# First 16 tokens' values with stacked high and low parts, and a later sub-norm, in a two-block f32 stack

## The chip, the cores and the metric

The kernel runs on one core of a Trainium2 chip. The metric is the device time of one launch in microseconds (us), as a median over runs. All matrix products are float32 products that are made on TensorE from pairs of float32r tiles: a high part and a low part of each operand, and three of the four products of the parts (high by high, high by low, low by high).

## The reference, cut to what matters

Two blocks run one after the other. Block 1 is two layers of ffn, token mixing and ffn on 512 tokens; block 2 puts 16 meta tokens in front and is two layers of a mixer and an ffn on 528 tokens. The model width is 1024. The change touches the values and forget logits of block 2's mixer, and the sub-norm of block 1's differential attention.

```
# block 2, mixer_sublayer (twice)
u = rms_norm(h, pre_g)                              # 528 x 1024
z = einsum("bld,de->ble", u, w_in)
q, k, v, f_logit, a_val, a_gate, sc_b, sc_c, sc_x = split(z)
log_f = log_sigmoid(f_logit + b_forget)             # 8 heads
y_attn = forgetting_attention(q, k, v, log_f)       # v: 528 x 512
a = causal_depthwise_conv(a_val * sigmoid(a_gate), a_dw_w) + a_dw_b   # 31 taps
...
# block 1, token_mixing (twice)
o_b = rmsnorm(diff_attention(...), subln_g) * (1.0 - lambda_init)
```

## The kernel before, in words

The residual lives transposed, 128 features by tokens, as eight chunks of the width (`KC` = 8). Block 2's 528 tokens are two halves: `H[0]` holds tokens 0 to 271 (the 16 meta tokens first), `H[1]` tokens 272 to 527. The normalized input of a sublayer is `xh` and `xl`, its high and low part, one pair of tiles for each chunk and half.

**Weights** are loaded by SyncE in 128x512 pieces (`wr`); ScalarE makes the high part (`wh`, L200) and VectorE the low part (`wl`, L201). A product is three matmuls for each chunk (`mm3`, L222 to L224; for values L778 to L780, where the tokens are the stationary operand and the weights stream).

**Values in mixer 2.** `gen_v(g)` (L1176) makes the values of four heads at a time. For g=0 the weight slice is 264 columns wide, 256 of values and 8 of forget logits; for g=1 it is 256. It hands a list of token blocks to `v_gen`: first the 16 meta tokens, then four blocks of 128. For each block and chunk there are three matmuls into one PSUM bank; then ScalarE writes the high part of the values (L787), VectorE the low part (L788), and for g=0 `forget` adds the bias to the logits (`lft`, L1166). So the 16 meta tokens cost 8 times 3 matmuls for each g, and there are two g and two layers. From the forget logits come `lf` (L1174), five small transposes (L1198), a scan (L1200), and the decay rows that go through DRAM (`fdram`, `dec`, L1202 and L1208) to the first scores (L1242).

**Order.** The program is a set of Python generators. They yield after each group of matmuls the TensorE time that they estimate (109 per matmul of values), and a planner takes the next piece from another generator when it is owed: the 31 taps of the depthwise convolution (L1333, L1337, one VectorE instruction each) are paced this way beside the values, and so are the filler matmuls of the next sublayer and the weight loads. Where a generator yields less, all that is paced by it comes earlier or later in the order of every engine.

**Sub-norm of block 1.** The differential attention's output is normed at the end of its units. Reciprocals are spread to 64 columns each (`bR`); after a yield, for each of four tiles two transposes on TensorE (L1063) bring them beside the output, VectorE scales (L1066), ScalarE and VectorE make the high and low parts (L1068, L1069). `SUBLN` says how many units of the other attention heads go by before each of the two parts is taken.

**GpSimd** (POOL) does next to nothing: a few memsets, and at the very end of the program eight residual additions (L370).

Of the kernel before, what the change touches and what calls it, by code (L numbers as in the profile page):

```python
# [9 lines left out]
F32 = mybir.dt.float32  # L10
F32R = mybir.dt.float32r
BF16 = mybir.dt.bfloat16
ACTF = mybir.ActivationFunctionType
ALU = mybir.AluOpType
# [3 lines left out]
KC = 8  # L18
# [4 lines left out]
HB = 272  # L23
# [17 lines left out]
END = (1050, 570)  # L41
CUT1, CUT2 = (7,), (5, 7)
OUT1, OUT2 = (5, 6, 7, 4, 3, 0, 1, 2), (0, 1, 4, 5, 2, 7, 6, 3)
SUBLN = (1, 2)
LATE = (3, 6, 7)
LAST = ("ffn3", DEPTH - 1)

# [32 lines left out]
def block_stack_kernel(ctx: ExitStack, tc: tile.TileContext, x_in, meta_in, vec_in, lam_in, wup1, wdn1, wqk1,  # L80
                       wv1, wo1, strip_a, wqk2, wv2, wcv2, wpw2, wo2, wup2, wdn2, c_ident, c_stripb,
                       c_cmask, c_fmask, c_sel, c_selc, out, n_sub=99):
    nc = tc.nc
    act, dve, pe, pool = nc.scalar, nc.vector, nc.tensor, nc.gpsimd
# [10 lines left out]
    def half(dt=F32, name="h"):  # L95
        return hp.tile([128, HB], dt, tag="h", name=name)
# [12 lines left out]
    def bank(tag, shape=(128, 512)):  # L109
        return ps.tile(list(shape), F32, tag=tag, bufs=bank_tags[tag], name="ps_" + tag)  # L110
# [4 lines left out]
    def lbank():  # L115

        lin[0] += 1
        return bank(lin[1][lin[0] % len(lin[1])])
# [8 lines left out]
    zeroc = one.tile([128, 1], F32, name="zeroc")  # L127
# [4 lines left out]
    def V(name, l, i=0, n=1):  # L132
        c = VCOL[name, l] + i
        return vec[:, c:c + n]
# [43 lines left out]
    def wunit(*key, back=0):  # L178

        assert plan[head[0]][0] == key, (plan[head[0]][0], key)  # L180
        head[0] += 1
        fetch(head[0] + AHEAD - back)
        return ready.pop(head[0] - 1)
# [19 lines left out]
    def fetch(to):  # L203
        while head[1] < min(to, len(plan)):
            for _ in load():
                pass
# [37 lines left out]
    class Whole:  # L244

        i, n, g, c = None, TALL - T0, slice(T0, TALL), slice(0, TALL - T0)
# [29 lines left out]
    def first_operand(opnd, h, g, wait):  # L276

        yield wait
        for c in range(KC):
            xs, gs = xT[:, c, h.g], g(c)  # L280
            xh, xl = opnd.tiles(c)
            act.activation(out=xh[:, h.g], in_=xs, func=ACTF.Copy, scale=gs)
            dve.scalar_tensor_tensor(out=xl[:, h.g], in0=xs, scalar=gs, in1=xh[:, h.g].bitcast(F32),  # L283
                                     op0=ALU.mult, op1=ALU.subtract)
            opnd.x[h.i, c] = (xh, xl)
            yield T_CH
        acc = None
        for c in range(KC):
            sq = half(name="sq")
            act.activation(out=sq[:, h.c], in_=xT[:, c, h.g], func=ACTF.Square)  # L290
            if acc is None:
                acc = sq
            else:
                dve.tensor_tensor(out=acc[:, h.c], in0=acc[:, h.c], in1=sq[:, h.c], op=ALU.add)
            yield T_SQ
        got = []
        yield from rb_steps(h, acc, got)
        opnd.set_rb(h, *got)
# [469 lines left out]
    def v_gen(opnd, us, tbs, width, get_v, extra=None, done=None):  # L768
        us = us() if callable(us) else us
        for (h, a, b, rcol) in tbs:  # L770
            n = b - a
            p = lbank()
            for c in range(KC):
                xh, xl = opnd.at(c)
                xsl = (slice(None), slice(a, b))
                wsl = (slice(None), slice((c % 4) * width, (c % 4 + 1) * width))
                wh, wl = us[c // 4]
                pe.matmul(out=p[:n, :width], lhsT=xh[xsl], rhs=wh[wsl], start=c == 0, stop=False)  # L778
                pe.matmul(out=p[:n, :width], lhsT=xh[xsl], rhs=wl[wsl], start=False, stop=False)
                pe.matmul(out=p[:n, :width], lhsT=xl[xsl], rhs=wh[wsl], start=False, stop=c == KC - 1)  # L780
                yield 3 * 109
            vt = get_v(a)
            r = opnd.r[h.i][:n, rcol:rcol + 1]
            vv = vt[:n].rearrange("p (q a b) -> p q a b", a=2, b=64)
            hi, lo = vv[:, :, 0, :], vv[:, :, 1, :]
            src = p[:n, 0:256].rearrange("p (q b) -> p q b", b=64)
            act.activation(out=hi, in_=src, func=ACTF.Copy, scale=r)  # L787
            dve.scalar_tensor_tensor(out=lo, in0=src, scalar=r, in1=hi.bitcast(F32), op0=ALU.mult,  # L788
                                     op1=ALU.subtract)
            if extra:  # L790
                extra(a, n, p, r)
            if done:
                done(a)
# [33 lines left out]
    def mixer1(l, opnd, gpost, nxt):  # L827
        H = HALF[1]
        li = 0.8 - 0.6 * math.exp(-0.3 * l)
        with ExitStack() as st:  # L830
# [261 lines left out]
            def with_subln(us):  # L1092

                sg = subln()
                for i, (needs, u) in enumerate(us):
                    def wrapped(u=u, i=i):
                        next(u)
                        yield
                        next(u)
                        if i in SUBLN:  # L1100
                            next(sg, None)
# [28 lines left out]
    def mixer2(l, opnd, gpost, nxt):  # L1130
        H = HALF[2]
        TB = [(0, 16), (16, 144), (144, 272), (272, 400), (400, 528)]
        with ExitStack() as st:
# [35 lines left out]
            def log_sigmoid():  # L1169
# [3 lines left out]
                act.activation(out=e, in_=e, func=ACTF.Ln, bias=1.0)  # L1173
                dve.scalar_tensor_tensor(out=f, in0=t, scalar=0.0, in1=e, op0=ALU.min, op1=ALU.subtract)  # L1174

            def gen_v(g):  # L1176
                w = 264 if g == 0 else 256
                us = lambda: [wunit("mix2", l, "v", g, j) for j in range(2)]

                def get(a):  # L1180
                    tb = 0 if a == 0 else (a - 16) // 128 + 1
                    vt[g, tb] = t = mp.tile([128, 512], F32R, tag="L", bufs=26, name="v")
                    return t
                tbs = [(H[0], 0, 16, 2)] + [(h, a, b, j) for h in H for j, (a, b) in enumerate(h.tb)]
                return v_gen(opnd, us, tbs, w, get, forget if g == 0 else None)

            def vsl(h, tb):
                m = TB[tb][1] - TB[tb][0]
# [307 lines left out]
            def run(gen, every):  # L1496

                ns = 0
                for d in gen:
                    ns += d  # L1500
                    while ns >= every:
                        fill(1)
                        ns -= every

            run(gen_v(0), TAP_V)
            log_sigmoid()
            first = pair(0)
# [6 lines left out]
            fl.add(("qk", 1), pair(1))  # L1514
            fl.add(("qk", 2), pair(2))
            fl.add(("v", 1), gen_v(1))
            fl.add("sc0", sc_branch(0))

# [11 lines left out]
            op = out_proj(2, l, ytile, gpost, nxt, OUT2, CUT2, y_done, scored)  # L1530
            fl.add("out", until_tail(op))
            us = []
# [87 lines left out]
    def blk_of(kind, l):  # L1620
        return 3 if (kind, l) == LAST else 2 if kind in ("mix2", "ffn3") else 1
# [3 lines left out]
    cur, opnd = None, Operand()  # L1625
# [17 lines left out]
    g = lambda c: V(pre[k0], l0, c)  # L1643
    start = iter([("steps", first_operand(opnd, h, g, T_B * h.i)) for h in HALF[blk_of(k0, l0)]])
    for i, (kind, l) in enumerate(subs):
        if i + 1 < len(subs):
            k2, l2 = subs[i + 1]
            nopnd = Operand()
            nxt = (HALF[blk_of(k2, l2)], nopnd, lambda c, k2=k2, l2=l2: V(pre[k2], l2, c))
        else:  # L1650
            nopnd = None
            nxt = (HALF[blk_of(kind, l)], None, None)
        gp = lambda c, kind=kind, l=l: V(post[kind], l, c)
        if kind == "mix1":
            gen = mixer1(l, opnd, gp, nxt)
        elif kind == "mix2":
            gen = mixer2(l, opnd, gp, nxt)
        elif kind == "ffn3":
            gen = ffn(blk_of(kind, l), (kind, l), opnd, gp, nxt, lambda f, l=l: V("ffn_conv_w_2", l, 3 * f, 3),
                      1 if blk_of(kind, l) == 3 else 2)  # L1660
        else:
            gen = ffn(1, (kind, l), opnd, gp, nxt)
        weave([cur or start, gen])
        if cur is None:
            prepare(*load_rest(g0))
        next(gen)
        cur, opnd = gen, nopnd
# [134 lines left out]
```

## Time and profile before

| | |
|---|---|
| median of 3 runs | 3420.25 us (3419.7 to 3424.2) |
| the profiled execution | 3422.85 us |
| its span, first to last instruction | 3421.1 us |
| mean granted TensorE clock | 0.991 of full |
| TensorE busy | 3381.2 us (99%) |
| weight loads on TensorE | 2992.2 us (87%) |
| VectorE busy | 2060.9 us (60%) |
| ScalarE busy | 1524.9 us (45%) |
| GpSimd busy | 8.9 us in 28 instructions |

How to read it: a row of the timeline is start, duration, engine, line, operation, output<-inputs, shape and count, with idle time and its releaser in brackets. Matmuls of a row overlap (each is shown with about 0.28 us while the next starts 0.12 us later), so what one costs is the distance between starts. A row of the windows is one stretch with the busy time and the number of instructions of each engine, the granted clock, and what the DMA moved. Names of tiles are the program's.

### The profile page before, as it was taken

The numbers are of one execution on the slowest core, as the hardware profiler recorded it, in microseconds if no ns is written. First come the engines' busy times: TensorE is split into PE (matmuls) and PEld (weight loads), VectorE is DVE, ScalarE is ACT, GpSimd is POOL, SyncE is SP. The second block draws the span as 40 slices with busy tenths as digits, with TensorE's granted clock in tenths as the row PEclk, the third lists the DMA queues.
The fourth block names the chain that finished last, engine by engine and source line by source line (L and its number), as shares of the span: only waits on it lengthen the run. The fifth ranks groups of instructions, "written<-read, shape, count | busy, mean of one in ns | idle before, by whom it ended". The sixth has DMA issues, their size and how long they took to land.

```text
span 3421.1 us, 55949 instructions
## 1 busy us (share of the span) xinstructions
PE 3381.2 (99%) x21765; PEld 2992.2 (87%) x21765; DVE 2060.9 (60%) x4433; ACT 1524.9 (45%) x3342; POOL 8.9 (0%) x28
## 2 busy tenths in 40 slices
PE   9999999999999999999999999999999999999998
PEld 8888987988888888987988898879999998799998
DVE  6442688744336442788744349768774397677743
ACT  6332566633234332566633235555443345664432
POOL 0000000000000000000000000000000000000000
PEclk9999999999999999999999999999999999999999
DMA  4223222232323223222223322102222221122222
GB/s 144 98 91 97 79 74 75 69 103 95 93 87 99 96 92 96 79 76 63 87 93 98 91 89 88 48 32 96 91 93 86 85 85 57 35 93 93 93 90 78
DMA packets 165817, 291.40 MB, mean 85 GB/s; under 512 B 19456, under 2 KB 36896, under 8 KB 165552
## 3 DMA queue, kind: packets, MB, share of 16 engines
q1 hardware_dynamic: 163648, 287.13, 26.4%
q8 instruction: 171, 2.80, 0.3%
q10 hardware_dynamic: 1904, 0.70, 0.1%
q14 instruction: 94, 0.77, 0.1%
HBM read 285.62 MB, written 2.13 MB: 84 GB/s over the span
## 4 chain that ended last, share of the span: by engine, by line
PE 88%; DVE 7%; ACT 3%; issue 1%; DMA 0%; SPq 0%; POOLq 0%; ACTq 0%; DVEq 0%
PE ps_acc L222 10%; PE ps_acc L223 10%; PE ps_acc L224 10%; PE ps_s L223 8%; PE ps_s L222 8%; PE ps_s L224 8%; PE ps_x L222 4%; PE ps_x L223 4%; PE ps_x L224 4%; PE ps_o L223 4%; PE ps_o L222 4%; PE ps_o L224 4%; PE ps_o L819 2%; PE ps_s L802 2%; DVE y L1337 1%
## 5 line engine op out<-in xcount | busy, mean ns | idle before, releaser
L200 ACT ACTIVATE wh<-wr 128x512 fp32r<-128x512 f32 (+2 forms) x1068 | 616.0, 615 | 1084.6 <-PE ps_acc L223 468.7
L201 DVE TENSOR_TENSOR wl<-wr,wh 128x512 fp32r<-128x512 f32 (+2 forms) x1068 | 693.1, 673 | 476.8 <-ACT wh L200 465.1
L222 PE MATMUL ps_acc<-xh,wh 128*128 128x256 f32 (+3 forms) x1608 | 533.5, 332 | 2.4 <-DVE qt L748 1.5
L223 PE MATMUL ps_acc<-xl,wh 128*128 128x256 f32 (+3 forms) x1608 | 521.4, 324 | 0.0
L224 PE MATMUL ps_acc<-xh,wl 128*128 128x256 f32 (+3 forms) x1608 | 521.1, 324 | 0.0
L223 PE MATMUL ps_s<-xl,wh 128*128 128x512 f32 (+3 forms) x1088 | 360.2, 331 | 2.8 <-DVE xl L283 0.8
L222 PE MATMUL ps_s<-xh,wh 128*128 128x512 f32 (+3 forms) x1088 | 357.5, 329 | 1.8 <-DVE z L531 1.6
L224 PE MATMUL ps_s<-xh,wl 128*128 128x512 f32 (+3 forms) x1088 | 356.5, 328 | 0.1
L222 PEld LDWEIGHTS ps_acc<-xh,wh 128*128 128x128 f32 x1608 | 306.4, 191 | 32.4 <-DVE qt L748 3.3
L224 PEld LDWEIGHTS ps_acc<-xh,wl 128*128 128x128 f32 x1608 | 306.0, 190 | 25.9 <-issue 1.5
L223 PEld LDWEIGHTS ps_acc<-xl,wh 128*128 128x128 f32 x1608 | 306.9, 191 | 22.1
L223 PEld LDWEIGHTS ps_s<-xl,wh 128*128 128x128 f32 x1088 | 204.8, 188 | 27.1 <-DVE xl L378 6.8
L222 PEld LDWEIGHTS ps_s<-xh,wh 128*128 128x128 f32 x1088 | 204.7, 188 | 22.2 <-DVE z L531 2.0
L224 PEld LDWEIGHTS ps_s<-xh,wl 128*128 128x128 f32 x1088 | 204.5, 188 | 18.7 <-DVE wl L201 0.3
L222 PE MATMUL ps_x<-xh,wh 128*128 128x256 f32 (+2 forms) x600 | 202.4, 337 | 0.0
L224 PE MATMUL ps_x<-xh,wl 128*128 128x256 f32 (+2 forms) x600 | 199.5, 333 | 0.0
L223 PE MATMUL ps_x<-xl,wh 128*128 128x256 f32 (+2 forms) x600 | 199.3, 332 | 0.0
L223 PE MATMUL ps_o<-xl,wh 128*128 128x512 f32 (+3 forms) x544 | 179.0, 329 | 1.0
L222 PE MATMUL ps_o<-xh,wh 128*128 128x512 f32 (+3 forms) x544 | 177.5, 326 | 0.1
L224 PE MATMUL ps_o<-xh,wl 128*128 128x512 f32 (+3 forms) x544 | 177.4, 326 | 0.0
L223 PE MATMUL ps_acc<-hl,wh 128*128 128x256 f32 (+1 forms) x528 | 168.5, 319 | 0.0
L222 PE MATMUL ps_acc<-hh,wh 128*128 128x256 f32 (+1 forms) x528 | 168.1, 318 | 0.0
(347 smaller groups left out, 7574.9 us busy)
## 6 DMA issues: line engine op xcount, KB each, us to landing
wr<-in_wup_dram SPq DMA_DIRECT2D x528, 256.0 KB, 2.8
wr<-in_wdn_dram SPq DMA_DIRECT2D x192, 256.0 KB, 2.7
wr<-in_wqk_dram SPq DMA_DIRECT2D x96, 256.0 KB, 2.8
wr<-in_wdn_dram SPq DMA_DIRECT2D x96, 192.0 KB, 2.6
wr<-in_wo_dram SPq DMA_DIRECT2D x64, 256.0 KB, 2.7
wr<-in_wv_dram SPq DMA_DIRECT2D x40, 256.0 KB, 2.9
wr<-in_wcv_dram SPq DMA_DIRECT2D x40, 256.0 KB, 2.8
dec<-fdram SPq DMA_DIRECT2D x16, 264.0 KB, 4.2
```

The costliest lines, as they stand in the source:

```text
L200: act.activation(out=hi[:, a:b], in_=raw[:, :b - a], func=ACTF.Copy)
L201: eng.tensor_tensor(out=lo[:, a:b], in0=raw[:, :b - a], in1=hi[:, a:b].bitcast(F32), op=ALU.subtract)
L222: pe.matmul(out=o, lhsT=wh[wsl], rhs=xh[xsl], start=start, stop=False)
L223: pe.matmul(out=o, lhsT=wh[wsl], rhs=xl[xsl], start=False, stop=False)
L224: pe.matmul(out=o, lhsT=wl[wsl], rhs=xh[xsl], start=False, stop=stop)
L802: pe.matmul(out=o, lhsT=a[R, qs], rhs=b[R, ks], start=j == 0, stop=j == 2 and mask is None)
L819: pe.matmul(out=o[:, q0:], lhsT=v, rhs=p[j], start=kb == 0 and j == 0, stop=kb == n - 1 and j == 1)
L1337: dve.scalar_tensor_tensor(out=y[:, s:], in0=t[0][:, :TALL - s], scalar=w[:, 30 - s:31 - s], in1=y[:, s:], op0=ALU.mult, op1=ALU.add))
```

## The change

The matmuls of the 16 meta tokens leave `v_gen`. A new generator, `first_v`, builds for each chunk a stationary operand of 48 columns, in which the 16 columns of the tokens' high part stand at 0 and the 16 of the low part at 32, with zeros between them and after; a matmul of that operand with the weights' high part gives high by high in rows 0 to 15 of the bank and low by high in rows 32 to 47. A second matmul, of the first 16 columns with the weights' low part, adds high by low to rows 0 to 15. So there are two matmuls for each chunk in place of three. GpSimd builds the operand: two fills with zero (128x272) and 16 copies (128x16) for each call, and `gen_v` is called four times. The two row groups are then added: ScalarE copies rows 32 to 47 to `vm`, VectorE adds rows 0 to 15, and the high and low parts of the values and the forget logits are made from `vm`. The generator yields 2*109 for each chunk. The second edit sets `SUBLN` from (1, 2) to (1, 3): the second part of the sub-norm is taken one unit later, in both layers of block 1.

```diff
--- before.py
+++ after.py
@@ -41,7 +41,7 @@
 END = (1050, 570)
 CUT1, CUT2 = (7,), (5, 7)
 OUT1, OUT2 = (5, 6, 7, 4, 3, 0, 1, 2), (0, 1, 4, 5, 2, 7, 6, 3)
-SUBLN = (1, 2)
+SUBLN = (1, 3)
 LATE = (3, 6, 7)
 LAST = ("ffn3", DEPTH - 1)
 
@@ -1173,16 +1173,51 @@
                 act.activation(out=e, in_=e, func=ACTF.Ln, bias=1.0)
                 dve.scalar_tensor_tensor(out=f, in0=t, scalar=0.0, in1=e, op0=ALU.min, op1=ALU.subtract)
 
+            def first_v(us, w, get, extra):
+
+                us, xm = us(), [half(F32R, "xm") for _ in range(2)]
+                for i in range(2):
+                    pool.tensor_copy(out=xm[i], in_=zeroc.to_broadcast([128, HB]))
+                    for c in range(4):
+                        for k in range(2):
+                            pool.tensor_copy(out=xm[i][:, 48 * c + 32 * k:48 * c + 32 * k + 16],
+                                             in_=opnd.at(4 * i + c)[k][:, 0:16].bitcast(F32))
+                p = lbank()
+                for c in range(KC):
+                    x = xm[c // 4][:, 48 * (c % 4):48 * (c % 4) + 48]
+                    wsl = (slice(None), slice((c % 4) * w, (c % 4 + 1) * w))
+                    wh, wl = us[c // 4]
+                    for rows, y in ((48, wh), (16, wl))[::-1 if c == KC - 1 else 1]:
+                        pe.matmul(out=p[:rows, :w], lhsT=x[:, :rows], rhs=y[wsl], start=c == 0 and rows == 48,
+                                  stop=c == KC - 1 and rows == 48)
+                    yield 2 * 109
+                t = half(name="vm")
+                act.activation(out=t[0:16, :w], in_=p[32:48, :w], func=ACTF.Copy)
+                dve.tensor_tensor(out=t[0:16, :w], in0=t[0:16, :w], in1=p[0:16, :w], op=ALU.add)
+                r = opnd.r[0][:16, 2:3]
+                vv = get(0)[:16].rearrange("p (q a b) -> p q a b", a=2, b=64)
+                src = t[:16, 0:256].rearrange("p (q b) -> p q b", b=64)
+                act.activation(out=vv[:, :, 0, :], in_=src, func=ACTF.Copy, scale=r)
+                dve.scalar_tensor_tensor(out=vv[:, :, 1, :], in0=src, scalar=r, in1=vv[:, :, 0, :].bitcast(F32),
+                                         op0=ALU.mult, op1=ALU.subtract)
+                if extra:
+                    extra(0, 16, t, r)
+
             def gen_v(g):
                 w = 264 if g == 0 else 256
-                us = lambda: [wunit("mix2", l, "v", g, j) for j in range(2)]
+                made = []
+
+                def units_of():
+                    made[:] = made or [wunit("mix2", l, "v", g, j) for j in range(2)]
+                    return made
 
                 def get(a):
                     tb = 0 if a == 0 else (a - 16) // 128 + 1
                     vt[g, tb] = t = mp.tile([128, 512], F32R, tag="L", bufs=26, name="v")
                     return t
-                tbs = [(H[0], 0, 16, 2)] + [(h, a, b, j) for h in H for j, (a, b) in enumerate(h.tb)]
-                return v_gen(opnd, us, tbs, w, get, forget if g == 0 else None)
+                tbs = [(h, a, b, j) for h in H for j, (a, b) in enumerate(h.tb)]
+                ex = forget if g == 0 else None
+                return itertools.chain(first_v(units_of, w, get, ex), v_gen(opnd, units_of, tbs, w, get, ex))
 
             def vsl(h, tb):
                 m = TB[tb][1] - TB[tb][0]
```

On TensorE, at the start of mixer 2's values in layer 0, the order before has the meta tokens' block first (`ps_o`, 24 matmuls of 16 rows, of which the first three stand here, the rest repeats them), behind the last product of the convolution's inputs:

```order
L222 MATMUL ps_x<-xh,wh 128x256
L223 MATMUL ps_x<-xl,wh 128x256
L326 MATMUL ps_t<-onec,sq 128x1 x2
L224 MATMUL ps_x<-xh,wl 128x256
L778 MATMUL ps_o<-wh,xh 16x264
L779 MATMUL ps_o<-wl,xh 16x264
L780 MATMUL ps_o<-wh,xl 16x264
```

Now a block of 128 tokens comes first and the 16 matmuls of `xm` follow it; these are the end of that block, two transposes of a reciprocal (L341), and the first chunk of `xm`:

```order
L778 MATMUL ps_acc<-wh,xh 128x264
L779 MATMUL ps_acc<-wl,xh 128x264
L780 MATMUL ps_acc<-wh,xl 128x264
L341 MATMUL ps_t<-ident,R 128x128 x2
L1191 MATMUL ps_o<-wh,xm 48x264
L1191 MATMUL ps_o<-wl,xm 16x264
```

Twenty-four rows became sixteen, and they moved behind the 24 of the first 128-token block.

On TensorE, in the first mixing layer of block 1, the sub-norm's four pairs of transposes stood between the score matmuls of a unit of 128 columns (L802):

```order
L802 MATMUL ps_s<-kh,qh 128x128 x2
L1063 MATMUL ps_t<-ident,bR 128x128 x2
L802 MATMUL ps_s<-kl,qh 128x128 x2
L1063 MATMUL ps_t<-ident,bR 128x128 x2
L802 MATMUL ps_s<-kh,ql 128x128 x2
L1063 MATMUL ps_t<-ident,bR 128x128 x2
L222 MATMUL ps_acc<-xh,wh 128x512
```

Now they stand behind the scores of the next unit, between products of the weights and the first of the values' products (L819):

```order
L802 MATMUL ps_s<-kh,ql 128x256 x2
L222 MATMUL ps_acc<-xh,wh 128x512
L1063 MATMUL ps_t<-ident,bR 128x128 x2
L223 MATMUL ps_acc<-xl,wh 128x512
L224 MATMUL ps_acc<-xh,wl 128x512
L1063 MATMUL ps_t<-ident,bR 128x128 x2
L222 MATMUL ps_acc<-xh,wh 128x512
L223 MATMUL ps_acc<-xl,wh 128x512
L224 MATMUL ps_acc<-xh,wl 128x512
```

The same rows move in the second layer.

On VectorE, between the convolution's input products and the forget gate (`lf`) of layer 0, the order before begins with both gatings of the convolution's input (L1330, two tiles) and the first tap (L1333):

```order
L1330 TENSOR_TENSOR av<-av,ag 128x528 x2
L1333 TENSOR_SCALAR y<-av,vec 128x528
L788 SCALAR_TENSOR_TENSOR v<-ps_o,rt,v 16x4x64
L1337 SCALAR_TENSOR_TENSOR y<-av,vec,y 128x527
L1166 SCALAR_TENSOR_TENSOR lft<-ps_o,rt,vec 16x8
```

Now only one gating stands there, and the addition of the row groups (L1196) is new; lines of the new kernel behind L1176 are 35 higher:

```order
L1365 TENSOR_TENSOR av<-av,ag 128x528
L1196 TENSOR_TENSOR vm<-vm,ps_o 16x264
L1368 TENSOR_SCALAR y<-av,vec 128x528
L1166 SCALAR_TENSOR_TENSOR lft<-vm,rt,vec 16x8
L1372 SCALAR_TENSOR_TENSOR y<-av,vec,y 128x527
L1201 SCALAR_TENSOR_TENSOR v<-vm,rt,v 16x4x64
```

The second gating now comes behind the first scores of the layer, and one tap fewer stands ahead of those scores.

## Rows read from the trace of the kernel before

**Rows 1.** Page, parts 1 and 4: busy time by engine; chain that ended last
```profile
PE 3381.2 (99%) x21765; PEld 2992.2 (87%) x21765; DVE 2060.9 (60%) x4433; ACT 1524.9 (45%) x3342; POOL 8.9 (0%) x28
...
PE 88%; DVE 7%; ACT 3%; issue 1%; DMA 0%; SPq 0%; POOLq 0%; ACTq 0%; DVEq 0%
```

**Rows 2.** Windows: us, busy by engine (instructions), PEclk, DMA share, GB/s
```profile
570.00:575.00 5.00, 4.10 (x24) 2.62 (x23) 4.81 (x12) 2.74 (x7) 0.00 (x0) 1.00 0.16 57
1585.00:1590.00 5.00, 4.56 (x27) 3.37 (x25) 3.98 (x11) 4.07 (x11) 0.00 (x0) 1.00 0.29 95
2050.00:2060.00 10.00, 9.56 (x68) 8.27 (x68) 9.19 (x28) 5.17 (x14) 0.00 (x0) 1.00 0.05 17
2083.00:2102.00 19.00, 18.67 (x150) 17.43 (x149) 18.78 (x36) 10.02 (x19) 0.34 (x2) 1.00 0.40 139
```

**Rows 3.** Timeline of PE: 16-token values of layer 0, g=0, then g=1
```profile
2067.66 0.28 PE L778 MATMUL ps_o<-wh,xh 128*16 128x264 f32 x1
...
2070.84 0.29 PE L778 MATMUL ps_acc<-wh,xh 128*128 128x264 f32 x1
...
2071.57 0.28 PE L778 MATMUL ps_acc<-wh,xh 128*128 128x264 f32 x1
...
2134.16 0.29 PE L778 MATMUL ps_acc<-wh,xh 128*16 128x256 f32 x1 [0.25 <-DVE qt L748]
...
2136.98 0.28 PE L778 MATMUL ps_acc<-wh,xh 128*128 128x256 f32 x1
```

**Rows 4.** Waits of PE over the whole span: us in total, times, longest
```profile
PE ps_t L1063 <- DVE ptl L906: 1.2, 2, 0.8
...
PE ps_o L1295 <- ACT sc L1251: 2.2, 1, 2.2
...
PE ps_t L1198 <- DVE lf L1174: 0.4, 2, 0.2
```

**Rows 5.** POOL instructions by form: count, busy us, mean ns, idle before
```profile
L370 POOL TENSOR_TENSOR xT<-xT,f 128x256 f32<-128x256 f32 x8 | 6.3, 786 | 621.1 <-DVE f L356 614.9 <-issue 6.2
L1596 POOL TENSOR_SCALAR vec<-vec 128x8 f32<-128x8 f32 x4 | 1.0, 289 | 4.0 <-DMA vec<-in_vec_dram 4.0
...
L1565 POOL MEMSET warm<- 128x272 f32 x1 | 0.3, 324 | 0.0
...
L1558 POOL MEMSET selz<- 128x16 f32 x1 | 0.1, 112 | 0.0
```

**Rows 6.** Groups of DVE instructions by form, 2050 to 2061 us
```profile
L378 DVE SCALAR_TENSOR_TENSOR xl<-xT,vec,xh 128x256 fp32r<-128x256 f32 x8 | 3.8, 473 | 0.7 <-ACT xh L386 0.7
L362 DVE TENSOR_TENSOR xT<-xT,f 128x256 f32<-128x256 f32 x8 | 3.3, 415 | 0.0
```

**Rows 7.** Timeline of DVE in mixer 2, layer 0
```profile
2072.44 1.33 DVE L1330 TENSOR_TENSOR av<-av,ag 128x528 f32<-128x528 f32 x2 [0.21 <-ACT ag L1329]
...
2074.15 0.47 DVE L788 SCALAR_TENSOR_TENSOR v<-ps_o,rt,v 16x256 fp32r<-16x256 f32 x1
2074.54 0.75 DVE L1337 SCALAR_TENSOR_TENSOR y<-av,vec,y 128x527 f32<-128x527 f32 x1
...
2081.96 1.29 DVE L201 TENSOR_TENSOR wl<-wr,wh 128x512 fp32r<-128x512 f32 x2 [1.19 <-ACT wh L200]
```

**Rows 8.** Timeline of SP and DVE: decay loads and their first use
```profile
2095.06 1.77 SPq L1208 DMA_DIRECT2D dec<-fdram  x4
...
2102.46 0.15 DVE L1242 CUSTOM_DVE_ANT_0 sc<-ps_s,dec 16x16 f32<-16x16 f32 x1
```

**Rows 9.** Timeline of POOL and DVE at the end of the program
```profile
3404.53 0.79 POOL L370 TENSOR_TENSOR xT<-xT,f 128x256 f32<-128x256 f32 x1 [614.07 <-DVE f L356]
...
3405.30 0.42 DVE L370 TENSOR_TENSOR xT<-xT,f 128x256 f32<-128x256 f32 x1
```

**Rows 10.** Windows at the end of layer 0's mixer 2
```profile
2285.00:2290.00 5.00, 2.91 (x10) 2.15 (x11) 4.34 (x9) 1.83 (x5) 0.00 (x0) 0.71 0.01 2
2290.00:2295.00 5.00, 5.00 (x22) 4.66 (x22) 1.38 (x4) 0.80 (x2) 0.00 (x0) 0.50 0.01 3
```

## The prediction, made before the changed kernel ran

> **What bounds the kernel now.** I read the page first: TensorE is busy 99% of the span, VectorE 60%, and 88% of the chain that ended last is TensorE [rows 1]. So an edit pays by the TensorE time that it takes out, if nothing else fills the gap, and a wait of TensorE on another engine is worth its length. Then I read the windows of the places that the diff touches. Around the sub-norm of block 1's first layer TensorE is busy 4.10 of 5 us, in the second layer 4.56 of 5 [rows 2]: small holes. Where mixer 2 begins, VectorE is busy 9.19 of 10 us (2050 to 2060), and behind the values 18.78 of 19 us (2083 to 2102) [rows 2]: there VectorE sets the pace beside TensorE, which still does 9.56 and 18.67. So the same saved TensorE time may be worth less there than elsewhere. Last come the waits of TensorE by line, and the clock by window.
>
> **The change, part by part.**
>
> *Fewer matmuls.* The meta tokens' 24 matmuls of layer 0 run from 2067.66 to 2070.84 us for g=0, with two transposes in between, and from 2134.16 to 2136.98 us for g=1 [rows 3]. The second gives 2.82 / 24 = 0.1175 us per matmul of 256 columns. The block of 128 tokens that follows the first has six matmuls in 2070.84 to 2071.57, or 0.122 us each for 264 columns [rows 3]. A stationary operand of 16 tokens and one of 128 thus cost the same within 5%; what counts is the columns that stream. So one of 48 columns costs no more, and the rival that the stacked matmul is dearer than the two that it replaces is shut out by these rows. Each call loses 8 of 24 matmuls: 8 x 0.122 + 8 x 0.1175 = 1.92 us per layer, 3.8 us in two layers. I take -3.8, with bounds of -3.8 (all of it reaches the end) and 0 (all of it turns into waits).
>
> *The join of the row groups.* Each call adds a ScalarE copy and a VectorE addition of 16 rows; the nearest row is the low part of the same 16 rows, 0.47 us [rows 7]. They lie off TensorE's path unless the forget gate is late. For g=0 the order helps: of the two gatings (1.33 us together) one now comes behind the first scores, and one tap of 0.75 us fewer stands ahead of them [rows 7]. Ahead of those scores VectorE has 0.67 + 0.75 - 0.47 = 0.95 us less to do, as much as TensorE saves there (8 x 0.122 = 0.98). Ahead of `lf` it has one tap more, one gating less and the addition: 0.75 - 0.67 + 0.47 = 0.55 us more. Against that, VectorE idles 1.19 us for a weight's high part in that stretch [rows 7]. TensorE waits for `lf` 0.2 us in each layer now [rows 4]; that wait may grow by 0 to 0.55 us. I take 0, as the idle time is larger than the added work.
>
> *The operand on GpSimd.* Eighteen instructions per call are new, on an engine that had 28 in all [rows 1]. No row shows this copy. From below 16 memsets of 128x16 and two of 128x272 would be 16 x 0.112 + 2 x 0.324 = 2.4 us; from above 16 of the 128x8 form and two additions of 128x256, 16 x 0.289 + 2 x 0.786 = 6.2 us [rows 5]. The chain begins, by what its tiles and sources wait for, near 2050 us in layer 0, and TensorE now wants it after the first 128-token block, about 2067.66 + 24 x 0.122 = 2070.6 us: 14 us to spare even at the upper end. For g=1 the chain comes behind the forget gate's tile, from about 2090 us, and is wanted at 2134. So nothing waits for it. What it may disturb is VectorE. In 2050 to 2061 us the eight chunks each have two VectorE instructions that read two tensors from SBUF, 0.47 and 0.42 us [rows 6], and the taps of 2083 to 2102 read two as well. At the end of the program GpSimd's additions run beside VectorE: one begins at 3404.53 and lasts 0.79, and VectorE's own L370, which reads two tensors, takes 0.42 [rows 9], as its twin L362 does alone [rows 6]. By this row nothing is lost; but the pair overlaps little, so it is a weak one. VectorE's loss lies between 0 and the whole chain of each call. I take 0.25 us per call, a tenth of the chain's lower end, because the row beside it shows none: +1.0 us over four calls.
>
> The Trainium skill, page "SBUF — State Buffer", section "Who interferes with whom", says that VectorE and GpSimd share one pair of ports that is locked, not split: a VectorE instruction with two SBUF inputs and a GpSimd instruction that reads SBUF exclude each other for a whole instruction. No row here shows such a stall. By that rule the first rival below would be the outcome.
>
> *Queues.* On SyncE two of the four `wv` loads now stand ahead of the four decay loads. Those four were issued from 2095.06 in 1.77 us, 0.44 each, and their first use is at 2102.46 [rows 8], 5.6 us behind the last issue. Two issues ahead of them cost 0.9, so 4.7 us remain for the landing. I take 0; if the cover were gone, TensorE would pay at most the 0.9 us in each layer.
>
> *The sub-norm a unit later.* TensorE waits 1.2 us in two places at L1063 for the previous transposes to be evacuated, 0.8 of it in one [rows 4]; with the neighbouring gaps the two windows show 0.90 and 0.44 us of idle time [rows 2]. In the new place the pairs stand between products of the weights, which can run while a bank is emptied. VectorE's work there only changes places, in a stretch where it is full (4.81 of 5 us [rows 2]), so a part may come back: from 0 to all of 1.3 us, or a little worse. I take -1.0, by the rows of the wait, since transposes between long matmuls have something to hide behind.
>
> *The sum.* -3.8 - 1.0 + 1.0 = -3.8 us against the profiled execution of 3422.85 us: 3419.05. That execution is 2.6 us above the median of the runs, so on the median **3416.5 us**, 0.11% faster. About 0.2%, 6.8 us, is what a measurement of this kernel can tell from no change; the forecast is within it.
>
> **The rivals.**
>
> *GpSimd holds VectorE up (the slower side).* Each of the 72 instructions stops VectorE for its length, since both places are full [rows 2]. Four chains at the lower price are 9.8 us, at the upper 24.8 us: 3420.25 - 4.8 + 9.8 = 3425 to 3440 us. It breaks even when a call costs VectorE 1.2 us, and the kernel is slower by over 0.2% from 2.9 us per call. For it speaks that VectorE paces TensorE in both stretches; against it the undisturbed 0.42 us at the end [rows 9], and that only copies which meet a two-tensor instruction count. Chance 0.14, of which 0.10 beyond 3427.1.
>
> *The saving is swallowed where VectorE is full.* The half that is saved for g=0 falls ahead of 2083 to 2102, where VectorE has no slack [rows 2]; if the later gating and tap do not give that back in time, TensorE waits for what it saved: only 1.9 of 3.8 us is kept, 3420.25 - 1.9 - 1.0 + 1.0 = 3418.4 us. For it: 18.78 of 19; against it: the 0.95 us that leave that stretch. Chance 0.22.
>
> *The clock, for the better.* At the end of each mixer TensorE idles (2.91 of 5 us busy), and in the window behind it the granted clock is 0.50, the 1.2 GHz level [rows 10]; five such microseconds cost 2.5 us of work. The single wait of 2.2 us there [rows 4] hangs on how much filler is left. The order of the whole mixer moves, so such a stretch may fall away in each layer: 3416.5 - 5.0 = 3411.5 us. Chance 0.16.
>
> *The clock, for the worse.* The filler that is used earlier lacks at the end, and one more such window comes in each layer: 3416.5 + 5.0 = 3421.5 us; with two in each layer 3426.5. Chance 0.12, of which 0.03 beyond 3427.1.
>
> **How the numbers follow.** The forecast has 0.36, with a range of its own of 3412 to 3420 us; 0.10 of it lies under 3413.4. Faster by over 0.2%: 0.10 + 0.16 = 0.26. Slower: 0.10 + 0.03 = 0.13. Within: 0.61. The range of 3408 to 3425 us takes in the better clock with some more, the swallowed saving, the worse clock once, and the lower end of the GpSimd rival; what is left out is the rest of that rival and the tails of the clock, under 0.2.
>
> **What would show it.** Right: 2 x 8 matmuls in each first-token block at 0.117 to 0.122 us apart; L1063 without a wait in the new place; the eight chunks of 2050 to 2060 us still with 0.47 and 0.42 us for VectorE's two-tensor instructions while GpSimd runs. Wrong: those instructions longer where GpSimd's copies stand, TensorE idle longer ahead of `lf` or the first scores, or more windows at a clock of 0.50 than before. If the change is over 7 us in either direction, the cause is one that I have only as a rival.

## The result and the profile after

The changed kernel takes 3438.99 us (median of 5 runs, 3434.95 to 3440.81), the kernel before 3419.87 (5 runs, 3418.53 to 3424.2): slower by 19 us, a ratio of 1.0052 (95% interval 1.0037 to 1.0066). The profiled execution has a span of 3437.0 us, 15.9 more than that of before. This is the page's first part:

```profile
PE 3388.5 (99%) x21733; PEld 2999.2 (87%) x21733; DVE 2064.2 (60%) x4437; ACT 1521.8 (44%) x3342; POOL 38.3 (1%) x100
```

TensorE has 32 instructions fewer, as the change says [rows 1]. Still it is busy 7.3 us longer, and span less busy time, its idle time, went from 39.9 to 48.5 us. So 8.6 of the 15.9 us are waits. The other 7.3 are matmuls that ran slower and, with the 3.8 us for the 32 that left, make some 11 us of slower matmuls. Busy time itself differs from execution to execution: two kernels below with the 24 matmuls, and in mixer 2 the order, of before are busy 3374.7 and 3376.0 us, where the profile of before has 3381.2, so against those the slower matmuls are worth 5 to 7 us more. The waits of TensorE over the whole span (us in total, times, longest) name where the first part is:

```profile
PE ps_acc L222 <- DVE y L1348: 6.6, 4, 3.1
PE ps_acc L222 <- DVE qt L748: 4.3, 4, 1.9
...
PE ps_t L1336 <- ACT sc L1286: 1.5, 2, 0.8
PE ps_t L1063 <- DVE ptl L906: 1.4, 2, 0.8
...
PE ps_t L1233 <- DVE lf L1174: 1.0, 2, 0.5
```

Before, the first two rows together were these:

```profile
PE ps_acc L222 <- DVE qt L748: 1.5, 4, 0.6
...
PE ps_acc L222 <- DVE y L1313: 0.6, 2, 0.3
```

They grew by 8.8 us. Four single waits, of 3.1 and 1.9 us, one of each in each layer of block 2, are 10.0 of the 10.9 us that the two rows now have. Both stand deep in mixer 2, at 2173 and 2228 us in layer 0, some 40 and 90 us behind the values of g=1. At the place of the first, the timeline of TensorE shows the filler product that takes over the two banks which VectorE empties as `y` (L222, eight chunks; the first half has 272 columns, the second 256). Before, its first matmul, a late one, and the second half's first:

```profile
2167.02 0.38 PE L802 MATMUL ps_s<-qh 64*128 64x256 f32 x1 [1.01 <-DVE y L1282]
...
2168.14 0.59 PE L222 MATMUL ps_acc<-xh,wh 128*128 128x272 f32 x1 [0.30 <-DVE y L1313]
...
2172.18 0.29 PE L222 MATMUL ps_acc<-xh,wh 128*128 128x272 f32 x1
...
2173.66 0.38 PE L222 MATMUL ps_acc<-xh,wh 128*128 128x256 f32 x1
```

After:

```profile
2166.52 0.39 PE L222 MATMUL ps_acc<-xh,wh 128*128 128x272 f32 x1 [0.20 <-DVE y L1348]
...
2168.85 0.38 PE L802 MATMUL ps_s<-qh 64*128 64x256 f32 x1
...
2170.02 0.29 PE L222 MATMUL ps_acc<-xh,wh 128*128 128x272 f32 x1
...
2173.64 0.38 PE L222 MATMUL ps_acc<-xh,wh 128*128 128x256 f32 x1 [3.08 <-DVE y L1348]
```

Now the product's first half begins 1.6 us earlier, ahead of the second pair of scores (L802) instead of behind it. TensorE could begin the second half at 2170.6 and stands until 2173.64. What it waits for is no earlier than it was. VectorE's timeline, before and after, has the two instructions that empty the banks; between them stand taps of the convolution (L1337, now L1372):

```profile
2167.66 0.43 DVE L1313 TENSOR_TENSOR y<-ps_acc,rb 128x272 f32<-128x272 f32 x1
...
2170.82 0.72 DVE L1337 SCALAR_TENSOR_TENSOR y<-av,vec,y 128x498 f32<-128x498 f32 x1
...
2172.68 0.41 DVE L1313 TENSOR_TENSOR y<-ps_acc,rb 128x256 f32<-128x256 f32 x1
```

```profile
2166.03 0.43 DVE L1348 TENSOR_TENSOR y<-ps_acc,rb 128x272 f32<-128x272 f32 x1
...
2172.53 0.72 DVE L1372 SCALAR_TENSOR_TENSOR y<-av,vec,y 128x498 f32<-128x498 f32 x1
2173.18 0.41 DVE L1348 TENSOR_TENSOR y<-ps_acc,rb 128x256 f32<-128x256 f32 x1
```

The slower matmuls are seen in the windows 70 us and more behind g=1's values (columns as in rows 2), first before and then after, in layer 0:

```profile
2205.00:2210.00 5.00, 5.00 (x38) 4.40 (x38) 4.21 (x12) 3.27 (x9) 0.00 (x0) 1.00 0.17 56
2210.00:2215.00 5.00, 4.14 (x27) 3.13 (x26) 3.89 (x13) 2.03 (x7) 0.00 (x0) 1.00 0.00 0
2215.00:2220.00 5.00, 5.00 (x29) 5.00 (x30) 3.63 (x14) 4.04 (x8) 0.00 (x0) 0.66 0.18 52
```

```profile
2205.00:2210.00 5.00, 5.00 (x26) 3.96 (x25) 2.46 (x5) 1.25 (x3) 0.00 (x0) 0.81 0.00 0
2210.00:2215.00 5.00, 5.00 (x22) 4.07 (x20) 2.23 (x7) 2.99 (x9) 0.00 (x0) 0.50 0.18 54
2215.00:2220.00 5.00, 5.00 (x21) 4.53 (x21) 4.10 (x12) 2.07 (x6) 0.00 (x0) 0.50 0.19 56
2220.00:2225.00 5.00, 5.00 (x30) 4.15 (x30) 1.78 (x6) 0.00 (x0) 0.00 (x0) 0.83 0.00 0
```

For some 14 us, 2208 to 2222, the granted clock was 0.50, 1.2 GHz; in layer 1 the same stretch comes at 2908 to 2922 us. Ahead of it, from 2180 to 2205 us, TensorE was at full clock and busy 4.51 to 5.00 of each 5 us.

At the places that the prediction names, little happened. The windows of rows 2, after:

```profile
570.00:575.00 5.00, 5.00 (x29) 3.88 (x28) 4.81 (x16) 3.18 (x10) 0.00 (x0) 1.00 0.15 53
1585.00:1590.00 5.00, 5.00 (x30) 3.90 (x29) 4.16 (x11) 3.73 (x10) 0.00 (x0) 1.00 0.26 90
2050.00:2060.00 10.00, 9.49 (x67) 8.17 (x66) 9.39 (x29) 5.83 (x16) 4.21 (x17) 1.00 0.01 2
2083.00:2102.00 19.00, 18.33 (x147) 17.05 (x146) 17.40 (x33) 8.98 (x16) 12.55 (x20) 1.00 0.38 114
```

The holes at the old place of the sub-norm are gone (5.00 of 5 in both), behind the values TensorE idles 0.67 us in place of 0.33, and in 2050 to 2060 us GpSimd works 4.21 us beside VectorE without a visible loss [rows 2]: the two-tensor instructions of the chunks take 0.47 and 0.41 us in the mean there, 0.47 and 0.42 before [rows 6]. The 16 matmuls of a call follow each other as foreseen:

```profile
2069.14 0.28 PE L1191 MATMUL ps_o<-wl,xm 128*16 128x264 f32 x1
2069.26 0.28 PE L1191 MATMUL ps_o<-wh,xm 128*48 128x264 f32 x1
2069.38 0.28 PE L1191 MATMUL ps_o<-wl,xm 128*16 128x264 f32 x1
```

### The profile page after: what moved, and what is told of

Same layout as the page of the kernel before. It is cut to its first block, busy times and chain, and to the rows that moved or that the text cites. A ratio compares the mean times of both kernels' runs of the same rounds, so it can differ in the third digit from the quotient of the medians.

```text
span 3437.0 us, 55998 instructions
## 1 busy us (share of the span) xinstructions
PE 3388.5 (99%) x21733; PEld 2999.2 (87%) x21733; DVE 2064.2 (60%) x4437; ACT 1521.8 (44%) x3342; POOL 38.3 (1%) x100
## 4 chain that ended last, share of the span: by engine, by line
PE 88%; DVE 7%; ACT 3%; issue 1%; DMA 1%; SPq 0%; POOLq 0%; ACTq 0%; DVEq 0%
PE ps_acc L222 10%; PE ps_acc L223 10%; PE ps_acc L224 10%; PE ps_s L223 8%; PE ps_s L222 8%; PE ps_s L224 8%; PE ps_x L222 4%; PE ps_x L223 4%; PE ps_x L224 4%; PE ps_o L223 4%; PE ps_o L222 4%; PE ps_o L224 4%; PE ps_s L802 2%; PE ps_o L819 1%; DVE y L1372 1%
## 5 line engine op out<-in xcount | busy, mean ns | idle before, releaser
L222 PE MATMUL ps_acc<-xh,wh 128*128 128x256 f32 (+3 forms) x1608 | 535.7, 333 | 10.9 <-DVE y L1348 6.6
L222 PE MATMUL ps_s<-xh,wh 128*128 128x512 f32 (+3 forms) x1088 | 357.3, 329 | 0.6 <-DVE z L531 0.5
L222 PEld LDWEIGHTS ps_acc<-xh,wh 128*128 128x128 f32 x1608 | 308.6, 192 | 41.3 <-DVE y L1348 7.3
L222 PEld LDWEIGHTS ps_s<-xh,wh 128*128 128x128 f32 x1088 | 204.6, 188 | 21.1 <-DVE z L531 0.9
L222 PE MATMUL ps_x<-xh,wh 128*128 128x256 f32 (+2 forms) x600 | 202.3, 337 | 0.0
L222 PE MATMUL ps_o<-xh,wh 128*128 128x512 f32 (+3 forms) x544 | 177.5, 326 | 0.1
L222 PE MATMUL ps_acc<-hh,wh 128*128 128x256 f32 (+1 forms) x528 | 168.1, 318 | 0.0
```

Source lines behind the costliest of these rows:

```text
L222: pe.matmul(out=o, lhsT=wh[wsl], rhs=xh[xsl], start=start, stop=False)
```

## The experiments

The theory: the smaller yield of the first 16 tokens moves what is paced by it, and that order makes the waits and the slow stretch (theory A). The rival: the new work itself, GpSimd's copies or the join (theory B). The four first kernels share their runs of the kernel before: 3419.43 us.

**The sub-norm alone.**

```diff
-SUBLN = (1, 2)
+SUBLN = (1, 3)
```

> The kernel before with the sub-norm a unit later and nothing else. The trace of the changed kernel has a VectorE instruction at 2048.38 us in the kernel before (the reciprocal of the norm) at 2047.59, 0.79 us earlier, and up to there only the sub-norm differs. Every theory expects a small gain from this edit: 0.5 to 1.5 us under the kernel before, about 3419. A value over 3422 would say that the later sub-norm is part of the loss.

3419.93 us, ratio 0.9999 (0.9991 to 1.0008): no difference that can be measured, and no gain shown. The row of the wait, in this kernel:

```profile
PE ps_t L1063 <- DVE ptl L906: 1.6, 2, 0.8
```

The wait was 1.2 us in two places [rows 4] and is 1.6. The kernel with unused copies below, which leaves the sub-norm where it was, has 1.6 too, so the wait neither grew nor shrank by the move: it moved with the transposes. In the changed kernel it is seen at the new place, where VectorE's work on the unit's own transposes is in front as it was at the old one:

```profile
578.00 0.41 PE L1063 MATMUL ps_t<-ident,bR 128*128 128x128 f32 x2 [0.82 <-DVE ptl L906]
```

**The values alone**, the changed kernel with

```diff
-SUBLN = (1, 3)
+SUBLN = (1, 2)
```

> The stacked first 16 tokens alone, sub-norm where it was. All theories that put the loss into mixer 2 expect the changed kernel's time plus about 0.8 us, 3436 to 3442. If it were 3420 to 3425, the two edits would only lose together.

3437.92 us, ratio 1.0051 (1.0039 to 1.0063). The loss is in mixer 2.

**The new work at the old pace, and the old work at the new pace.** The first is the changed kernel with

```diff
-                    yield 2 * 109
+                    yield 3 * 109
```

> The changed kernel in which the first 16 tokens' generator yields 3 x 109 for each chunk, as before, so that taps and filler are paced as before; the work is that of the changed kernel. Theory A (pacing): the smaller yield pulls the filler of the values of g=1 forward and moves the taps, and that makes the waits of 3.1 and 1.9 us and the new stretch at half clock in each layer: they go, and the time is 3414 to 3421. Theory B (the new work itself: GpSimd's copies beside VectorE, the added VectorE and ScalarE instructions on a late chain): the time stays at 3433 to 3442.

and the second the kernel before with

```diff
-                yield 3 * 109
+                yield (2 if n == 16 else 3) * 109
```

> The kernel before, with its 24 matmuls for the first 16 tokens, in which only the yield of that block is 2 x 109 in place of 3 x 109; no GpSimd work, no stacked operand. Theory A (pacing): most of the loss comes back, 3430 to 3442, with a wait of about 3 us on the convolution's y product and a half-clock stretch in each layer. Theory B (new work): no loss, 3418 to 3423.

The first takes 3423.87 us (1.0014, 1.0005 to 1.0022), the second 3432.67 (1.0043, 1.0029 to 1.0057; its runs lie between 3426.3 and 3440.04). So a number in a `yield`, with no instruction added or removed, makes most of the loss. The waits of the second kernel are those of the changed one to the tenth:

```profile
PE ps_acc L222 <- DVE y L1313: 6.6, 4, 3.1
PE ps_acc L222 <- DVE qt L748: 4.3, 4, 1.9
```

Its stretch at half clock stands at 2205 to 2225 us too, in layer 0; in layer 1 of this profile no window of the place is below 0.79. The profiled execution, 3427.21 us, is one of three at 3426 to 3429 us, with a mean granted clock of 0.992; the other three took 3436 to 3440 us, with 0.987 to 0.989. So with one and the same order the time at half clock differs from execution to execution. Theory A holds; but the first kernel is still 4.4 us above the kernel before where 4.8 us less was due by my terms for the matmuls and the sub-norm, so something of the new work costs.

**Which yield.** The next four share 3419.38 us for the kernel before. In the changed kernel the old yield for one `g` alone:

```diff
-                    yield 2 * 109
+                    yield (2 if w == 264 else 3) * 109
```

> The changed kernel, with the old yield of 3 x 109 for the first 16 tokens of g=1 alone; for g=0 it stays at 2 x 109 (one tap fewer beside the values). If the filler that g=1's shorter values pull forward makes the big waits (3.1 us on the convolution's y, 1.9 us on qt, the stretch at half clock behind them), they are gone here: 3420 to 3427, as with the old yield for both (3423.9). If the tap of g=0 makes them, the time stays at 3433 to 3441.

and the mirror:

```diff
-                    yield 2 * 109
+                    yield (3 if w == 264 else 2) * 109
```

> The mirror: the old yield for g=0 alone, 2 x 109 for g=1. If g=1's filler makes the big waits, they stay, 3433 to 3441; if g=0's tap does, 3420 to 3427.

3419.29 us (1.0000, 0.9991 to 1.0009) and 3435.25 us (1.0053, 1.0040 to 1.0065). It is g=1: its values are a piece of filler, fed by the planner in TensorE time, and 8 x 109 less of it pulls everything behind it in the same list forward. For g=0 the smaller yield is even the better one: with the old yield for both the ratio is 1.0014, with the old one for g=1 alone 1.0000, each against its own runs of the kernel before. There the yield sets how many taps VectorE gets beside the values, and with one tap more TensorE waits in the full stretch; this row of the timeline stands in the kernel with the old yield for both (0.60 us in layer 1), and no such wait over 0.2 us at this place in the other:

```profile
2097.44 0.39 PE L222 MATMUL ps_acc<-xh,wh 128*128 128x256 f32 x1 [0.79 <-DVE qt L748]
```

These 1.4 us are a part of the some 4.6 between the two kernels. What makes the rest is not shown: in the two profiles TensorE's idle time differs by only 0.7 us, its busy time by 3.1.

**The copies alone.** The kernel before, in which the function that fetches the values' weights also makes the two tiles, and nobody reads them:

```diff
+                def us():
+                    copies()
+                    return [wunit("mix2", l, "v", g, j) for j in range(2)]
+
+                def copies():
+                    xm = [half(F32R, "xm") for _ in range(2)]
...
+                                pool.tensor_copy(out=xm[i][:, 48 * c + 32 * k:48 * c + 32 * k + 16],
+                                                 in_=opnd.at(4 * i + c)[k][:, 0:16].bitcast(F32))
```

> The kernel before in the same order on every other engine, with GpSimd's four times 18 fills and copies added and their result read by nobody. Theory: GpSimd is the one that waits when it meets VectorE (its copies take 0.19 us in the trace of the changed kernel where VectorE is free, up to 3.76 us beside the taps, while a tap still takes 0.74 to 0.75 us), so the time is that of the kernel before within 1.5 us, 3418 to 3421. Rival (my first rival of the prediction): VectorE is held up, by 9.8 us at the least, 3429 or more; a part of it, 3422 to 3428, if only the stretch at 2050 us pays.

3419.54 us, 0.9999 (0.9990 to 1.0008). GpSimd costs nothing here that can be measured. The timelines of the changed kernel show why: one copy at the boundary, four behind the values, and VectorE's instructions that run there.

```profile
2052.11 0.19 POOL L1183 CAST xm<-xl 128x16 fp32r<-128x16 f32 x1
...
2092.24 3.76 POOL L1183 CAST xm<-xl 128x16 fp32r<-128x16 f32 x1
2095.96 0.68 POOL L1183 CAST xm<-xh 128x16 fp32r<-128x16 f32 x1
2096.59 0.20 POOL L1183 CAST xm<-xl 128x16 fp32r<-128x16 f32 x1
2096.73 1.28 POOL L1183 CAST xm<-xh 128x16 fp32r<-128x16 f32 x1
```

```profile
2090.32 0.90 DVE L1372 SCALAR_TENSOR_TENSOR y<-av,vec,y 128x513 f32<-128x513 f32 x1
...
2091.50 0.74 DVE L1372 SCALAR_TENSOR_TENSOR y<-av,vec,y 128x512 f32<-128x512 f32 x1
...
2093.33 0.71 DVE L1372 SCALAR_TENSOR_TENSOR y<-av,vec,y 128x511 f32<-128x511 f32 x1
...
2096.51 0.42 DVE L748 TENSOR_TENSOR qt<-ps_acc,rb 128x272 f32<-128x272 f32 x1
```

A copy that takes 0.19 us takes up to 3.76 where VectorE is full, and the taps take 0.74 and 0.71 us, about as before [rows 7]. One tap of this stretch takes 0.90, here and in the kernel with the unused copies: so VectorE is held up by 0.16 us, GpSimd by some 8 us. The eight copies of this stretch that take 0.19 or 0.20 us lie beside `qt` (L748), which reads one tile of SBUF and one bank of PSUM, or where VectorE is idle; the long ones lie beside instructions that read two tiles of SBUF, the longest over several of them. The rule of the Trainium skill, page "SBUF — State Buffer", section "Who interferes with whom", that a VectorE instruction with two SBUF inputs and a GpSimd instruction that reads SBUF exclude each other, agrees with these rows. That VectorE is the one that waits, as the prediction took it, does not follow from that rule; here it was mostly GpSimd, which has 30 us to spare for g=1.

**The stacked operand for g=1 alone**, at the old yield, with the later sub-norm:

```diff
-                    yield 2 * 109
+                    yield 3 * 109
...
+                if g == 0:
+                    return v_gen(opnd, units_of, [(H[0], 0, 16, 2)] + tbs, w, get, ex)
```

> The stacked operand for g=1 alone, with the old yield; for g=0 the 24 matmuls first, as before; sub-norm a unit later. 16 matmuls fewer, 1.9 us. If what the changed kernel with the old yield still loses (3423.9 where 3415.6 was due) comes from the values of g=0 (forget gate later, weight loads ahead of the decay rows), this one is at 3416 to 3419. If it comes from g=1 (the wait for the first scores' exponentials in front of its values, 0.76 us per layer) or from the order in general, it is at 3420 to 3424.

3417.58 us, 0.9995 (0.9986 to 1.0004): the lowest median of all, but not told apart from the kernel before. It is the outcome that was expected if the loss that the old yield for both leaves (ratio 1.0014) comes from the values of g=0.

What became of the 3.8 us is seen in the kernel with the old yield for g=1, whose time is that of the kernel before. Its timeline of TensorE at the forget gate and at g=1's values:

```profile
2091.02 0.71 PE L1233 MATMUL ps_t<-ident,lf 16*8 16x16 f32 x5 [0.51 <-DVE lf L1174]
...
2135.35 0.66 PE L1336 MATMUL ps_t<-ident,sc 128*128 128x128 f32 x4 [0.76 <-ACT sc L1286]
```

The wait for `lf` is 0.51 us (0.2 before [rows 4]). And in front of g=1's values TensorE waits 0.76 us for exponentials, where before it waited 0.25 us, for `qt` [rows 3]: of the eight transposes of the scores (L1301, now L1336) four stood before the first 16 tokens' matmuls and four behind them, at 2138.75 us; now all eight stand before. The 2.8 us of matmuls that covered ScalarE's exponentials no longer stand in between. The two together are 0.32 + 0.51 = 0.8 us per layer of the 1.9 saved. In that profile the same matmuls of layer 0 lie 0.76 us behind those of the profile before at 2052 us and 0.71 behind at 2192 and 2272, so nothing of the 1.9 is left in the end. Some 0.5 of the other 1.1 goes at the first scores: the same matmuls are 0.15 us behind at 2099 us and 0.63 behind at 2104.8. In between VectorE waits 0.43 and 0.30 us for decay rows, and TensorE waits for VectorE's results of these scores at this place in layer 1, 0.27 and 0.28 us. The rest I have not followed up.

**How the time hangs on g=1's yield.** The last four share 3418.93 us. In the kernel before, with its 24 matmuls, only this changes:

```diff
-                yield 3 * 109
+                yield 218 if n == 16 and width == 256 else 3 * 109
```

and 272, 382 and 436 in place of 218.

> The kernel before with its 24 matmuls; only the first 16 tokens of g=1 yield 2 x 109 for each chunk. If this yield alone makes the loss, without stacked operand, copies, join or later sub-norm, the time is 3430 to 3440 (the changed kernel: 3439; old yield for g=1 alone: 3419.3). If g=0's yield or the new work has a part in it, 3422 to 3430.

> As the last, with 272 for each chunk (two and a half matmuls): the filler comes forward by half as much. If the loss grows evenly with the shift, some 3427; if it hangs on whole products of the filler that change sides with the scores, it is either near 3420 or near 3436.

> The other way: 382 for each chunk, the filler comes later by half of that shift. If only a filler that comes too early costs (TensorE runs ahead of VectorE's y), 3417 to 3421; if any shift from the given order costs, 3424 or more.

> 436 for each chunk, the filler later by the whole shift. Same two theories: 3417 to 3421 if only early filler costs, 3425 or more if any shift does.

| yield for each chunk | us | ratio (95% interval) |
|---|---|---|
| 218 | 3435.68 | 1.0049 (1.0037 to 1.0062) |
| 272 | 3424.01 | 1.0014 (1.0005 to 1.0023) |
| 327 (before) | 3418.93 | |
| 382 | 3423.21 | 1.0008 (1.0000 to 1.0017) |
| 436 | 3424.08 | 1.0011 (1.0003 to 1.0020) |

The first makes most of the loss by itself, about 17 of 19 us. Against the two kernels that have the same matmuls and in mixer 2 the order of before (the sub-norm alone, the unused copies), TensorE is idle 5 to 7 us longer in its profile and busy 11 to 13 us longer. Its waits, and at 436 a row of the other kind:

```profile
PE ps_acc L222 <- DVE y L1313: 5.3, 4, 2.4
PE ps_acc L222 <- DVE qt L748: 4.2, 4, 1.9
```

```profile
2171.73 0.59 PE L222 MATMUL ps_acc<-xh,wh 128*128 128x272 f32 x1 [3.59 <-DVE y L1313]
```

Filler that comes later makes a wait as well, 3.6 us on the first half of the same product. So I was wrong with both simple forms, that only early filler costs and that it costs in one step: each of the three smaller or later shifts is slower by 0.08 to 0.14%, 3 to 5 us (at 382 the interval reaches to no change), and the full shift forward, which alone of the four brings the 1.9 us wait and the stretch at half clock with it, costs 17.

## Why the prediction was wrong

The term that failed is one that the sum does not have: the smaller yield. The order of rows at mixer 2's start was read, and the taps of g=0 counted, but for g=1 only the matmuls were costed; that its yield feeds the filler, and that a filler product 40 us later would change places with the scores, had no price. Earlier filler stands in the prediction only as a reason for the clock rival. The yield of g=1 is worth about 17 us, more than all other terms together.

- *Fewer matmuls, -3.8 us.* The durations were right: 0.12 us from start to start with 16, 48 or 128 stationary columns. The saving was not: with the loss taken out, 3419.29 against 3419.38 us. The rival of the swallowed saving had the right kind, for g=0; for g=1 the cover of the exponentials, which the removed matmuls were, stood in no term.
- *The join, 0 us, bounded by 0.55 at `lf`.* The wait grew by 0.3 us in each layer, inside the bounds.
- *GpSimd beside VectorE, +1.0 us.* Nothing: 0.9999. A copy alone takes 0.19 us, inside the bounds of 0.112 and 0.289. The rival in which VectorE is held up by every copy for its length is refuted by the kernel with unused copies: one tap grows by 0.16 us, and it is the copies that stretch.
- *The queue of SyncE, 0 us.* This term was too small. The decay rows landed 6.2 us behind their issue, in the median of all 16 loads (before 4.2), and the cover was 4.7 us. VectorE waited for them 0.22 us in layer 0 and up to 1.10 in layer 1, and TensorE behind it for the results `mn` of these scores; over the span that wait grew from 0.3 to 1.9 us, some 0.8 a layer and within the 0.9 that the prediction allowed. How much of it is due to the rows is not shown: in the kernel with the old yield for both it is 1.5, with no wait for decay rows in the profile.

```profile
2102.99 0.16 DVE L1277 CUSTOM_DVE_ANT_0 sc<-ps_s,dec 16x16 f32<-16x16 f32 x1 [0.22 <-DMA dec<-fdram]
...
2802.48 0.16 DVE L1277 CUSTOM_DVE_ANT_0 sc<-ps_s,dec 16x16 f32<-16x16 f32 x1 [1.10 <-DMA dec<-fdram]
```

```profile
2803.06 0.36 PE L802 MATMUL ps_s<-qh 64*128 64x272 f32 x1 [0.36 <-DVE mn L1277]
```

- *The sub-norm, -1.0 us.* Not measurable; the wait of 0.8 us at the old place stands at the new place with 0.82. It is a wait for VectorE's work on the attention unit's own transposes, and the next unit has it too.
- *The clock, for the worse.* The direction was right and the place near, the size was not: I priced one or two windows in each layer at the end of the mixer; there came a stretch of 14 us in its middle, worth half of that, 7 us in each layer, some 5 more than what the window at 0.66 cost there before, and other stretches left. As far as the runs show it comes with the early filler: the changed kernel and the four in which g=1 yields 2 x 109 have it at 2205 to 2225 us, and none of the others has a window at 0.50 there. In layer 1 it is missing in one of the four, so the order makes it possible and does not fix it. What in the order brings it about was not tried.

The range ended at 3425 us and the time is 3439: not a bound that was too narrow, but a mechanism that was missing. The 0.13 for slower rested on GpSimd and the clock alone.

## What to carry to other kernels

Where generators yield their cost and a planner deals out other work by it, the number in the `yield` is part of the schedule: when the work behind it shrinks, time the shorter work at the old pace first, and change the pace as an edit of its own, for each generator alone (here the old pace was right for g=1, the new one for g=0). In an order fitted to its numbers, look not only at the edited place but for every piece of work that is paced by it, and price the first place where it changes sides with a chain of another engine. And matmuls that are saved in front of a wait are worth only what exceeds that wait.

## What the runs showed of the hardware that was not expected

GpSimd's small copies (128x16) took 0.19 or 0.20 us where VectorE was idle or read one tile of SBUF, and up to 3.76 us beside a stream of VectorE instructions that read two. Of the taps in that stretch one took 0.90 us in place of 0.74, and the others kept their length. GpSimd was busy 12.55 us in the 19 us of 2083 to 2102 for work that takes about 4 alone (16 x 0.19 and 0.98 for the fills at 2049.55), and the kernel with the unused copies was no slower. Work on GpSimd that has time to spare was thus free in this kernel; no run here has such work that another engine waits for.
